# Products over 64 and 32 rows of the array made over all rows, and the output projection in chunks of 512, 320 and 256 columns, in a hybrid decoder step

## The chip, the core and the metric

The kernel runs on one core of a Trainium2 chip. The core has TensorE (PE in the profile; its loads of weights are PEld), VectorE (DVE), ScalarE (ACT), GpSimd (POOL) and SyncE (SP), which issues nearly all transfers. The metric is the device time of one execution in microseconds (us).

## The reference, cut to what matters

One layer of a decoder (D_MODEL 2048) for a prompt of 1024 tokens and for 8 sequences of 8 new tokens (64 in all; 1088 tokens together):

```python
h = rmsnorm(x) * (1 + scale) + shift                 # scale, shift, gate from silu(c) @ ada_w
q_a, k_a, v_a, z_a, u_b, v_b, z_b, qk_c, v_c, o_c, z_c, i_c, f_c = split(h @ w_in)
# A, 12 heads of 64: q, k normalised in each head; three dilated windows with relative bias,
#    combined by their softmax denominators; times silu(z_a)
# B, spatial gating: u * (tril(w_s) @ rmsnorm(v) + b_s) * silu(z_b)
# C, mLSTM, 6 heads of 128: short causal conv on q/k, chunkwise recurrence with
C_new = wc * C + einsum('bhs,bshk,bshv->bhkv', ws, k, v)
x = x + gate * (concat(y_a, y_b, y_c) @ w_out)
```

All of it is in float32. It returns the new x, and the new windows, buffers and states.

## The kernel before, in words

Data lies with features on the 128 partitions and the 1088 tokens along the row. Large products are made of three: an operand is split into a high part, rounded to the format that TensorE multiplies at the higher rate (float32r, FR in the code), and a low part, the rest; high*high + high*low + low*high are added in one PSUM bank. `products` (L249) issues these three, lines 252, 253 and 254, for one block of 128 input features and one chunk of tokens. The tokens are cut into three chunks, `CH` (L25): 384, 384 and 320.

ACT rounds the high part of a weight piece (L98), POOL makes the low part (L99), both two pieces ahead; SP loads pieces still further ahead (L87).

Stages in order: norm and modulation, with the first columns of the input projection accumulated as the modulation arrives (to 200 us); columns of the input projection (`column`, L602: a tile of 128 output features over four weight pieces and three chunks); the mLSTM heads beside later columns (to 1215 us); spatial gating; the attention of the new tokens against the cache, beside further columns (1525 to 1910 us); the first part of the output projection (features 6 to 15 of `yD`, `project`, L1586) with the prompt's attention woven in (to some 2395 us); the second part (features 0 to 5, the attention's own output).

The order is written out by hand. After each group of products `tick` (L179) lets background work take steps: `hp` one step at each tick, `lp` `rate` steps (0.345 a tick in the first part of the projection). Work in `lp` is written as generators, and each `yield` ends a step. Each engine works off its own instructions in this order, so a step fixes only the order, and semaphores the rest. Stores are put off by some ticks (`later`, L157).

Products over fewer than 128 rows that the diff touches:

- Norm factors of q and k, `rms` (L757). The sums of squares of both heads of a tile end up at rows 32c and 32c+1 of chunk c, 96 rows for the three chunks (L762); DVE takes the inverse root, keeps it as a rounded and a remaining part in the rows 32c to 32c+3 (`yc`, L781), and a product with the selector `sel` (L787), over the 32 rows of the chunk, spreads it over the 128 features. `sel` is 96 x 128 (L258), loaded at the very start (L263). Twelve tiles, three chunks.
- States of the new tokens, in `mlstm` (L909): the update of the state for four sequences at once, 512 columns. `kwh` holds the high part of the weighted keys twice, in rows 0 to 63 and 64 to 127; `vm` holds the values, high part above, low part below; L1032 multiplies over 128 rows, L1033 multiplies the low part of the keys, `kwl` (64 rows), with the upper half of `vm`. Six heads, two halves.
- Scores of the prompt's attention, `scores` (L1428): `qs` holds the high part of q in rows 0 to 63 and its low part in 64 to 127; `kd` holds the high part of k twice. L1442 makes high*high + low*high over 128 rows, L1443 adds high*low over rows 0 to 63 with `kl` (L1403). Columns: up to 512 keys, at least 256. 144 such pairs, 12 for each of the 12 heads.

Around the scores, in one step: the products of probabilities with values, L1493 and L1495, for an earlier block; the scores of a block; the transposes of an earlier block's probabilities (`turn`, L1470, L1484); then what is due (exp, scaling L1459, the low part `pL` of the transposed probabilities L1486). `prep` (L1383) loads and splits keys, queries and values of the next head, for heads after the first on POOL (L1403, L1408, L1414).

`project` (L1586) keeps three PSUM banks, one for each chunk, and `residual` (L1575) adds gate * result to x, in the last chunk with a part of its own for the 64 new tokens.

Other lines named later: L276 and L762 (sums of squares), L346 and L357 (modulation), L1242 and L1292 (scores and values of the new tokens), all of which write 32 output partitions; L287 to L289 (transposes of 96, 64 and 32 rows in `token_rsqrt`); L1061 (transposes in `mlstm`).

Of the kernel before, what the change touches and what calls it, by code (L numbers as in the profile page):

```python
# [11 lines left out]
FT = mybir.dt.float32  # L12
FR = mybir.dt.float32r
# [98 lines left out]
def body(tc, I, O):  # L112
# [20 lines left out]
    def et(name="e"):  # L133
        return ev.tile([128, 388], FT, tag="e", name=name, bufs=7)
# [122 lines left out]
    gate = cp.tile([128, KT, ND9], FT, name="gate")  # L257
    sel = cp.tile([96, 128], FR, name="sel")  # L258
    knew = cp.tile([128, 2, 2, NSM], FT, name="knew")
    qg8 = cp.tile([128, 1], FT, name="qg8")  # L260
    V.tensor_scalar(qg8, C("qg"), 0.125, None, op0=OP.mult)
    t = et("sel")
    SP.dma_start(t[:96, :128], I["sel"][:96])  # L263
    V.tensor_copy(sel, t[:96, :128])

# [489 lines left out]


    def rms(cc, g, emit):  # L757

        yield
        ps = bank("rq")  # L760
        for c, (t0, n) in enumerate(CH):
            T.matmul(ps[32 * c:32 * c + 32, :n], C("half"), cc[c][1][:, :n], start=True, stop=True, skip_group_check=True)  # L762
        a = cc[0][1]
        V.tensor_scalar(a[0:64, :384], ps[0:64, :384], 1.0 / 64, EPS, op0=OP.mult, op1=OP.add)
        V.tensor_scalar(a[64:96, :320], ps[64:96, :320], 1.0 / 64, EPS, op0=OP.mult, op1=OP.add)
        V.memset(a[64:96, 320:384], 1.0)
        y, t = et("y")[:96, :384], et("t")[:96, :384]
        a = a[:96, :384]
        V.tensor_scalar(y.bitcast(I32), a.bitcast(I32), -0.5, 1597463007.0, op0=OP.mult, op1=OP.add)
        for i in range(3):  # L770
            if i < 2:
                yield
            V.tensor_tensor(t, y, y, op=OP.mult)
            V.scalar_tensor_tensor(t, t, -0.5, a, op0=OP.mult, op1=OP.mult)
            V.scalar_tensor_tensor(y, t, 1.5, y, op0=OP.add, op1=OP.mult)

        yh, yc = (ev.tile([128, 388], FR, tag="e", name=x, bufs=7)[:96, :384] for x in ("yh", "yc"))
        yield
        S.copy(yh, y)
        yield  # L780
        V.scalar_tensor_tensor(yc, y, C("low", rows=96), yh.bitcast(FT), op0=OP.mult, op1=OP.subtract)  # L781
        yield
        for c, (t0, n) in enumerate(CH):
            raw = cc[c][0]
            ps = bank("rb")
            r = slice(32 * c, 32 * c + 32)
            T.matmul(ps[:, :n], sel[r, :], yc[r, :n], start=True, stop=True)  # L787
            V.scalar_tensor_tensor(raw[:, :n], raw[:, :n], g, ps[:, :n], op0=OP.mult, op1=OP.mult)
            emit(c, raw, t0, n)
            yield  # L790
# [45 lines left out]
    pcv = mp_.tile([128, 12, 3], FT, name="pcv")  # L836
    scv = mp_.tile([128, 12, NB, 3], FT, name="scv")
    pnt = mp_.tile([128, HC], FT, name="pnt")
# [31 lines left out]
    def h_qk(h, isk):  # L870
# [3 lines left out]
        def f(c, ps, t0, n):  # L874
# [19 lines left out]
            if c == 2:  # L894
# [4 lines left out]
                for j in range(1, 4):  # L899
                    V.scalar_tensor_tensor(us, Rs[:, :, j:j + NT], cw[:, m, j:j + 1], us, op0=OP.mult, op1=OP.add)  # L900
                V.tensor_copy(scv[:, m], Rs[:, :, 8:11])
            S.activation(t[:, :n], u[:, :n], AF.Tanh)
# [6 lines left out]
    def mlstm(h):  # L909
# [97 lines left out]
        kv = ev.tile([128, 388], FR, tag="e", name="kvp", bufs=7)  # L1007
        kwh, vns, kwl = kv[:, 0:128], kv[:, 128:256], kv[:p, 256:384]
        S.copy(kwh[:p], kw[:p])
# [5 lines left out]
        T.matmul(b3[:, 256:264], kw[:p], C("bm01", rows=p), start=True, stop=True)  # L1015
        V.tensor_tensor(kwl, kw[:p], kwh[:p].bitcast(FT), op=OP.subtract)
        V.tensor_tensor(vns[p:], vn[:p, :128], vns[:p].bitcast(FT), op=OP.subtract)
# [4 lines left out]
        for i in range(2):  # L1022
# [9 lines left out]
            T.matmul(b3, kwh, v2, start=True, stop=False)  # L1032
            T.matmul(b3, kwl, v2[:p], start=False, stop=True)  # L1033
            V.tensor_tensor(c, c, b3.rearrange("p (b v) -> p b v", b=4), op=OP.add)
# [46 lines left out]
    for p in range(2, 4):  # L1081
        column(col["va", p], h_va(p))
    column(col["ka", 0], h_qka(0, True))
    drain(lp)
    later(lambda: (SP.dma_start(O["p_conv"], pcv), SP.dma_start(O["s_conv"], scv),
                   SP.dma_start(O["p_n"], pnt), SP.dma_start(O["s_n"], snt)))
# [126 lines left out]
    def sample(qd):  # L1213
# [18 lines left out]
        for hf in range(2):  # L1232
# [65 lines left out]
            for b in range(4):  # L1298
                T.matmul(os_[32 * b:32 * b + 32, :256], pts[5][:NSM, 32 * b:32 * b + 32], vn, start=False, stop=True,
                         skip_group_check=True)  # L1300
            ost = ap_.tile([128, 256], FT, tag="ost", name="ost", bufs=1)
            S.copy(ost, os_[:, :256])
# [80 lines left out]
    def prep(hd):  # L1383
# [18 lines left out]
        S.copy(kd[:, :NPR], kr[:, :NPR])  # L1402
        E.tensor_tensor(kl[0:64, :NPR], kr[0:64, :NPR], kd[0:64, :NPR].bitcast(FT), op=OP.subtract)  # L1403
        e["kd"], e["kl"] = kd, kl
# [23 lines left out]
    def scores(e, m):  # L1428

        P = []  # L1430
        for r in range(2):
# [6 lines left out]
            for k0 in range(0, nk, 512):  # L1438
# [3 lines left out]
                T.matmul(ps[:, :wide], e["qs"][:, a], e["kd"][:, k0:k0 + wide], start=True, stop=False)  # L1442
                T.matmul(ps[:, :wide], e["qs"][0:64, a], e["kl"][0:64, k0:k0 + wide], start=False, stop=True)  # L1443
                x = k0 + 896 - 128 * qb
# [122 lines left out]
    def loads(ks):  # L1567
        for j, k in enumerate(ks):
# [4 lines left out]
            load_y(k, G)  # L1573

    def residual(x, c, ps, t0, n, dm):  # L1575
        npr = n if c < 2 else n - NSM
# [9 lines left out]
    def project(pieces, src, dst):  # L1586
        for dm in range(KT):
# [3 lines left out]
            for q, (k0, nk) in enumerate(pieces):  # L1591
                wh, wl = W.get()
                last = q == len(pieces) - 1
                for c, (t0, n) in enumerate(CH):
                    if q == 0:
# [187 lines left out]
```

## Time and profile before

| | |
|---|---|
| median of 3 runs | 2551.05 us (2546.61 to 2551.82) |
| the profiled execution, whole | 2550.13 us |
| its span, first to last instruction | 2548.4 us |
| TensorE busy in the span | 2499.6 us (98%) |
| DVE, ACT, POOL busy | 940.8, 746.1, 645.7 us (37%, 29%, 25%) |
| mean granted clock of TensorE | 0.995 |
| matmuls | 15879 |

How to read it: a row of the timeline gives the start in us from the span's start, the duration in us, the engine, the line of the kernel, the operation, output<-inputs by their names in the program, and for a matmul rows*columns of the loaded weights, then rows x columns of the moving operand; x4 is four in a row, merged. Matmuls overlap: the next one starts before the one ahead has ended, so their durations add up to more than the time. In the row of granted clocks each digit is a fortieth of the span, in tenths. In a list of waits a row is: who waited, line, for whom, us in total, times, the longest.

### The profile page before, as it was taken

Reading aid. Unit: us, or ns where it says so; the run is one execution under the profiler, and the core shown is the slowest. Engines: PE = TensorE matmul, PEld = TensorE weight load, DVE = VectorE, ACT = ScalarE, POOL = GpSimd, SP = SyncE. Lnnn points to the kernel's source line nnn. Section 1 sums busy time; section 2 is a strip of 40 time slices with the busy share of each in tenths; the row PEclk is TensorE's granted clock in tenths of the full one; section 3 lists DMA queues with packets and bytes.
Section 4 is the critical chain, followed back from the end, with each engine's and each line's share of the span. In section 5 each row is a group of like instructions: output and inputs, shape, how many; then the busy total and the mean of one; then the engine's idle time right before and its main releaser. Section 6 shows DMA issues by size and latency. Waiting matters only on the chain.

```text
span 2548.4 us, 39820 instructions
## 1 busy us (share of the span) xinstructions
PE 2499.6 (98%) x15879; PEld 2264.7 (89%) x15879; DVE 940.8 (37%) x2480; ACT 746.1 (29%) x1638; POOL 645.7 (25%) x502
## 2 busy tenths in 40 slices
PE   5999999999999999999999999999999999999999
PEld 2677899999999999999899998888889888888999
DVE  4673001323232323232440003333113777777322
ACT  3222212323232323223221112222113555555210
POOL 2541123222323131312212221111111323232421
PEclk8999999999999999999999999999999999999999
DMA  8864611111112111112314327475657455444454
GB/s 282 283 215 157 216 57 38 60 55 59 60 55 65 55 60 55 56 59 78 96 59 132 113 89 257 170 235 198 232 181 229 120 137 143 141 140 131 146 170 144
DMA packets 157081, 332.95 MB, mean 131 GB/s; under 512 B 21770, under 2 KB 76962, under 8 KB 149216
## 3 DMA queue, kind: packets, MB, share of 16 engines
q1 hardware_dynamic: 156896, 330.41, 40.0%
q8 instruction: 125, 2.05, 0.3%
q14 instruction: 60, 0.49, 0.1%
HBM read 284.26 MB, written 54.55 MB: 133 GB/s over the span
## 4 chain that ended last, share of the span: by engine, by line
PE 93%; DMA 3%; DVE 3%; issue 0%; SPq 0%; ACT 0%; POOL 0%; DVEq 0%; ACTq 0%; POOLq 0%
PE mm L252 26%; PE mm L254 25%; PE mm L253 25%; PE pt L1484 2%; PE s L1443 2%; PE ad L346 2%; PE os L1292 1%; PE s L1442 1%; PE sq L1242 1%; PE o L1495 1%; PE o L1493 1%; DMA x<-in_xT 1%; PE rb L787 1%; DMA ad<-in_adaw 0%; PE b L936 0%; PE b L968 0%
## 5 line engine op out<-in xcount | busy, mean ns | idle before, releaser
L252 PE MATMUL mm<-hH,wh 128*128 128x384 f32 (+1 forms) x3168 | 1066.5, 337 | 10.5 <-ACT hH L429 8.5
L253 PE MATMUL mm<-hL,wh 128*128 128x384 f32 (+1 forms) x3168 | 1034.9, 327 | 2.5 <-DVE hL L435 2.5
L254 PE MATMUL mm<-hH,wl 128*128 128x384 f32 (+1 forms) x3168 | 1036.3, 327 | 0.0
L99 POOL TENSOR_TENSOR wl<-wraw,wh 128x512 fp32r<-128x512 f32 x344 | 444.0, 1298 | 1619.8 <-ACT wh L98 1477.1
L252 PEld LDWEIGHTS mm<-hH,wh 128*128 128x128 f32 x3168 | 595.4, 188 | 80.9 <-issue 46.4
L253 PEld LDWEIGHTS mm<-hL,wh 128*128 128x128 f32 x3168 | 595.9, 188 | 4.2 <-DVE hL L435 3.6
L254 PEld LDWEIGHTS mm<-hH,wl 128*128 128x128 f32 x3168 | 595.1, 188 | 0.0
L98 ACT CAST wh<-wraw 128x512 fp32r<-128x512 f32 x344 | 200.9, 596 | 381.8 <-PE mm L253 276.6
L252 PE MATMUL mm<-yH,wh 128*128 128x384 f32 (+1 forms) x768 | 264.3, 344 | 2.8 <-DVE xo L1577 2.8
L254 PE MATMUL mm<-yH,wl 128*128 128x384 f32 (+1 forms) x768 | 252.2, 328 | 0.6 <-POOL wl L99 0.6
L253 PE MATMUL mm<-yL,wh 128*128 128x384 f32 (+1 forms) x768 | 251.8, 328 | 0.0
L252 PEld LDWEIGHTS mm<-yH,wh 128*128 128x128 f32 x768 | 145.1, 189 | 6.1 <-issue 5.9
L254 PEld LDWEIGHTS mm<-yH,wl 128*128 128x128 f32 x768 | 145.0, 189 | 0.9 <-POOL wl L99 0.9
L253 PEld LDWEIGHTS mm<-yL,wh 128*128 128x128 f32 x768 | 145.6, 190 | 0.0
L892 DVE SCALAR_TENSOR_TENSOR u<-R,cw,u 128x384 f32<-128x384 f32 (+1 forms) x108 | 62.0, 574 | 213.3 <-ACT u L890 210.8
L1485 ACT CAST pH<-pt 128x512 fp32r<-128x512 f32 (+1 forms) x120 | 65.2, 544 | 125.3 <-PE pt L1484 124.4
L1577 DVE SCALAR_TENSOR_TENSOR xo<-mm,gate,xo 128x384 f32<-128x384 f32 (+1 forms) x96 | 54.3, 569 | 117.0 <-PE mm L254 116.7
L1486 DVE TENSOR_TENSOR pL<-pt,pH 128x512 fp32r<-128x512 f32 (+1 forms) x120 | 75.3, 628 | 17.0 <-ACT pH L1485 15.0
L1484 PE MATMUL pt<-cst,P 128*128 128x128 f32 x432 | 75.0, 290 | 3.1 <-DVE P L1459 2.6
L1445 DVE CUSTOM_DVE_ANT_0 P<-s,btab 128x512 f32<-128x512 f32 (+2 forms) x96 | 56.4, 587 | 57.0 <-PE s L1443 54.9
L1454 ACT ACTIVATE P<-P,mx 128x128 f32<-128x128 f32 (+3 forms) x96 | 74.4, 776 | 4.0 <-DVE mx L1451 2.1
L1484 PEld LDWEIGHTS pt<-cst,P 128*128 128x128 f32 x432 | 45.9, 141 | 27.9 <-issue 17.2
(323 smaller groups left out, 2422.4 us busy)
## 6 DMA issues: line engine op xcount, KB each, us to landing
wraw<-in_win SPq DMA_DIRECT2D x264, 256.0 KB
ad<-in_adaw SPq DMA_DIRECT2D x96, 512.0 KB
kv<-in_ck SPq DMA_DIRECT2D x30, 1024.0 KB
kv<-in_cv SPq DMA_DIRECT2D x30, 1024.0 KB
wraw<-in_wout SPq DMA_DIRECT2D x48, 256.0 KB
x<-in_xT SPq DMA_DIRECT2D x16, 544.0 KB
yraw<-yD SPq DMA_DIRECT2D x16, 544.0 KB
xo<-in_xT SPq DMA_DIRECT2D x16, 544.0 KB
```

The costliest lines, as they stand in the source:

```text
L98: self.nc.scalar.copy(wh[:, :n], raw[:, :n])
L99: self.nc.gpsimd.tensor_tensor(wl[:, :n], raw[:, :n], wh[:, :n].bitcast(FT), op=OP.subtract)
L252: T.matmul(ps[:, :n], wh[:, a], rh[:, t0:t0 + n], start=first and i == 0, stop=False)
L253: T.matmul(ps[:, :n], wh[:, a], rl[:, t0:t0 + n], start=False, stop=False)
L254: T.matmul(ps[:, :n], wl[:, a], rh[:, t0:t0 + n], start=False, stop=last and i == len(rows) - 1)
L892: V.scalar_tensor_tensor(u[:, :npr], R[:, j:j + npr], cw[:, m, j:j + 1], u[:, :npr], op0=OP.mult, op1=OP.add)
L1445: V.tensor_tensor_reduce(s[:, k0:k0 + w], ps[:, :w], e["bt"][:, x:x + w], 1.0, mx[:, np_ - 1:np_] if np_ else -3.0e38, op0=OP.add, op1=OP.max,
L1454: S.activation(s[:, :nk], s[:, :nk], AF.Exp, bias=mx[:, 2:3], accum_out=mx[:, 3:4])
L1484: T.transpose(pt[:, o:o + 128], P[r][:, k:k + 128], ident)
L1485: S.copy(pH[:, f:], pt[:, f:])
L1486: at(0, 3, lambda: V.tensor_tensor(pL[:, f:], pt[:, f:], pH[:, f:].bitcast(FT), op=OP.subtract))
L1577: V.scalar_tensor_tensor(x[:, t0:t0 + npr], ps[:, :npr], gate[:, dm, 0:1], x[:, t0:t0 + npr], op0=OP.mult, op1=OP.add)
```

## The change

It makes three kinds of product over all rows of the array instead of a part of them, and cuts the projection's chunks otherwise.

- `sel` becomes three blocks of 96 x 128, each zero but for the 32 rows of its chunk; L787 then multiplies over all 96 rows. `sel` is loaded, zeroed and filled after the start stage's memory is given back (about 305 us in the profile before) instead of at the start.
- `kwl` is made for both halves of the rows, so L1033 multiplies over 128 rows (the low part of the keys times the low part of the values comes in besides).
- `kl` is made for 128 rows, so L1443 multiplies over 128 rows (low*low comes in besides).
- `project` uses `CO`, chunks of 512, 320 and 256, instead of `CH`.
- For room: the updated conv buffer is written in place (`sconv` instead of `scv`), and `ost` takes a buffer of the ring `pt`.

```diff
-    sel = cp.tile([96, 128], FR, name="sel")
-    t = et("sel")
-    SP.dma_start(t[:96, :128], I["sel"][:96])
-    V.tensor_copy(sel, t[:96, :128])
@@ after st0.close()
+    sel = pool("qk", bgs, bufs=1).tile([96, 3, 128], FR, name="sel")
+    t = et("sel")
+    SP.dma_start(t[:96, :128], I["sel"][:96])
+    V.memset(sel.bitcast(FT), 0.0)
+    for c in range(3):
+        r = slice(32 * c, 32 * c + 32)
+        V.tensor_copy(sel[r, c, :], t[r, :128])
@@ rms
-            r = slice(32 * c, 32 * c + 32)
-            T.matmul(ps[:, :n], sel[r, :], yc[r, :n], start=True, stop=True)
+            T.matmul(ps[:, :n], sel[:, c, :], yc[:, :n], start=True, stop=True)
@@ h_qk
-                V.tensor_copy(scv[:, m], Rs[:, :, 8:11])
+                V.tensor_copy(sconv[:, m], Rs[:, :, 8:11])
@@ mlstm
-        kwh, vns, kwl = kv[:, 0:128], kv[:, 128:256], kv[:p, 256:384]
+        kwh, vns, kwl = kv[:, 0:128], kv[:, 128:256], kv[:, 256:384]
-        V.tensor_tensor(kwl, kw[:p], kwh[:p].bitcast(FT), op=OP.subtract)
+        for r in (slice(0, p), slice(p, 128)):
+            V.tensor_tensor(kwl[r], kw[:p], kwh[:p].bitcast(FT), op=OP.subtract)
-            T.matmul(b3, kwl, v2[:p], start=False, stop=True)
+            T.matmul(b3, kwl, v2, start=False, stop=True)
@@ sample
-            ost = ap_.tile([128, 256], FT, tag="ost", name="ost", bufs=1)
+            ost = ap_.tile([128, 256], FT, tag="pt", name="ost", bufs=3)
@@ prep
-        E.tensor_tensor(kl[0:64, :NPR], kr[0:64, :NPR], kd[0:64, :NPR].bitcast(FT), op=OP.subtract)
+        E.tensor_tensor(kl[:, :NPR], kr[:, :NPR], kd[:, :NPR].bitcast(FT), op=OP.subtract)
@@ scores
-                T.matmul(ps[:, :wide], e["qs"][0:64, a], e["kl"][0:64, k0:k0 + wide], start=False, stop=True)
+                T.matmul(ps[:, :wide], e["qs"][:, a], e["kl"][:, k0:k0 + wide], start=False, stop=True)
@@ project
+    CO = ((0, 512), (512, 320), (832, 256))
-                for c, (t0, n) in enumerate(CH):
+                for c, (t0, n) in enumerate(CO):
```

More of the change, by code (lines that the diff above doesn't have):

```diff
@@ L836, in body @@
     pcv = mp_.tile([128, 12, 3], FT, name="pcv")
-    scv = mp_.tile([128, 12, NB, 3], FT, name="scv")
     pnt = mp_.tile([128, HC], FT, name="pnt")
@@ L1084, in body @@
     drain(lp)
-    later(lambda: (SP.dma_start(O["p_conv"], pcv), SP.dma_start(O["s_conv"], scv),
+    later(lambda: (SP.dma_start(O["p_conv"], pcv), SP.dma_start(O["s_conv"], sconv),
                    SP.dma_start(O["p_n"], pnt), SP.dma_start(O["s_n"], snt)))
```

## The prediction

> **What bounds the kernel now.** I read the page first: the busy shares, the row of granted clocks, then the waits of TensorE, then the timeline of TensorE around every kind of product that the diff touches.
>
> ```profile
> span 2548.4 us, 39820 instructions
> PE 2499.6 (98%) x15879; PEld 2264.7 (89%) x15879; DVE 940.8 (37%) x2480; ACT 746.1 (29%) x1638; POOL 645.7 (25%) x502
> PEclk8999999999999999999999999999999999999999
> ```
>
> TensorE is busy 98% of the span at nearly full granted clock. A busy PE isn't a PE at its peak, so the question is what lies inside the busy time. The waits of TensorE over the stage where prompt attention is woven into the first part of the output projection (1955 to 2395 us), and the engines' busy time there:
>
> ```profile
> PE mm L252 <- DVE xo L1577: 2.8, 1, 2.8
> PE pt L1484 <- DVE P L1459: 2.6, 3, 1.5
> PE o L1495 <- DVE pL L1486: 0.8, 3, 0.4
> ```
>
> ```profile
> 1960.00:2395.00 435.00, 429.23 (x2515) 369.19 (x2516) 311.05 (x922) 241.36 (x495) 130.18 (x83) 0.99 0.49 139
> ```
>
> The columns of the second are the stretch, then busy us and instructions of PE, PEld, DVE, ACT and POOL, the clock, the DMA share and GB/s. TensorE waits for others some 6 us in 440; everything else that it loses, it loses to itself. So I price each product by the distance from its start to the next start, which the timeline gives, and not by its duration (a matmul that lasts 0.33 us starts 0.17 us after the one before). The measure for undisturbed products, from the second part of the projection, fifteen products of 384 columns and then twelve of 320:
>
> ```profile
> 2537.01 0.33 PE L252 MATMUL mm<-yH,wh 128*128 128x384 f32 x1
> ...
> 2539.61 0.31 PE L252 MATMUL mm<-yH,wh 128*128 128x320 f32 x1
> ...
> 2541.36 0.34 PE L252 MATMUL mm<-yH,wh 128*128 128x384 f32 x1
> ```
>
> (2539.61 - 2537.01)/15 = 0.173 us for 384 columns, (2541.36 - 2539.61)/12 = 0.146 for 320: 0.0275 per 64 columns. Carried on, that gives 0.228 for 512 and 0.118 for 256 (an estimate for 512: no undisturbed one is in the trace).
>
> **The change part by part.** (a) Norm factors, L787, 32 rows. How many of each touched product there are, and one of them with its neighbours (rows*columns of the loaded weights, then rows x moving columns):
>
> ```profile
> L787 PE MATMUL rb<-yc,sel x36: 403/436/442, 1226.1 to 1787.0; 32*128 32x384 f32 x24, 32*128 32x320 f32 x12
> L1443 PE MATMUL s<-kl,qs x144: 379/466/501, 1964.8 to 2356.8; 64*128 64x512 f32 x72, 64*128 64x256 f32 x48, 64*128 64x384 f32 x24
> L1033 PE MATMUL b<-vm,kvp x12: 492/498/502, 512.6 to 1187.3; 64*128 64x512 f32 x12
> ```
>
> ```profile
> 1225.88 0.31 PE L254 MATMUL mm<-hH,wl 128*128 128x320 f32 x1
> 1226.12 0.44 PE L787 MATMUL rb<-yc,sel 32*128 32x384 f32 x1
> 1226.49 0.45 PE L252 MATMUL mm<-hH,wh 128*128 128x384 f32 x1
> 1226.77 0.34 PE L253 MATMUL mm<-hL,wh 128*128 128x384 f32 x1
> ```
>
> Three distances are too long. Before it: 0.24 where 0.146 is due (+0.094). Its own: 0.37 for 0.173 (+0.197). The one behind: 0.28 for 0.173 (+0.107). Together 0.40 us for one product over 32 rows, besides its own stream. After the change the product has 96 rows. Does 96 still count as a part of the array? The trace has one product over 96 rows behind a full one:
>
> ```profile
> 1241.09 0.34 PE L254 MATMUL mm<-hH,wl 128*128 128x384 f32 x1
> 1241.27 0.33 PE L287 MATMUL tr<-cst,ts 96*128 96x96 f32 x2
> ```
>
> 0.18 us before it, as between full ones; so I take 96 rows as full. Along the timeline 15 of the 36 are followed by a full product of the projection (0.40 each: 6.0 us), 9 by full products of 128 columns, behind which the third distance is over by 0.06 only, as (b) shows (0.35 each: 3.2), and 12 by products into 32 output columns. Those have a distance of their own in front:
>
> ```profile
> 1528.32 0.34 PE L254 MATMUL mm<-hH,wl 128*128 128x384 f32 x1
> 1528.59 1.07 PE L1242 MATMUL sq<-kv,qst 128*32 128x256 f32 x16
> ```
>
> 0.27 where 0.173 is due. So of the 0.197 behind these twelve L787 only 0.10 goes, and 0.09 ahead: 0.19 each, 2.3 us. Sum of (a): 11.5 us.
>
> (b) Scores, L1443, 64 rows. One pair of 512 columns with four transposes behind it, the same four transposes behind a full product, and one pair of 384 columns with a projection product behind it:
>
> ```profile
> 2202.58 0.40 PE L1442 MATMUL s<-kd,qs 128*128 128x512 f32 x1
> 2202.90 0.50 PE L1443 MATMUL s<-kl,qs 64*128 64x512 f32 x1
> 2203.33 0.66 PE L1484 MATMUL pt<-cst,P 128*128 128x128 f32 x4
> 2203.75 0.42 PE L252 MATMUL mm<-yH,wh 128*128 128x384 f32 x1
> ```
>
> ```profile
> 525.70 0.34 PE L254 MATMUL mm<-hH,wl 128*128 128x384 f32 x1
> 525.87 0.60 PE L1061 MATMUL b<-cst,kT 128*128 128x128 f32 x4
> 526.23 0.43 PE L252 MATMUL mm<-hH,wh 128*128 128x384 f32 x1
> ```
>
> ```profile
> 2196.89 0.28 PE L1495 MATMUL o<-pL,vh 128*64 128x256 f32 x1
> 2197.01 0.34 PE L1442 MATMUL s<-kd,qs 128*128 128x384 f32 x1
> 2197.28 0.43 PE L1443 MATMUL s<-kl,qs 64*128 64x384 f32 x1
> 2197.64 0.44 PE L252 MATMUL mm<-yH,wh 128*128 128x384 f32 x1
> 2197.92 0.34 PE L253 MATMUL mm<-yL,wh 128*128 128x384 f32 x1
> ```
>
> With transposes behind: L1442 to L1443 0.32 for 0.228, L1443 to L1484 0.43 for 0.228, the four transposes 0.42 for 0.36: +0.09, +0.20, +0.06, in all 0.35. With a projection product or the next pair behind: 0.27 for 0.173, 0.36 for 0.173, 0.28 for 0.173: in all 0.39. Counted along the timeline, 115 of the 144 are of the first kind and 29 of the second: 40.3 + 11.3 = 51.6 us. The full-row L1443 itself costs what L1442 costs: the columns are the same. L1495 (128 rows, 64 columns of weights) has 0.12 behind it, which is undisturbed, so it isn't touched and needn't be.
>
> (c) States, L1033, 64 rows, 512 columns, projection products behind: 0.09 + 0.20 + 0.11 = 0.40, twelve times, 4.8 us.
>
> So 11.5 + 51.6 + 4.8 = 67.9 us come off TensorE, and since TensorE is the end of nearly every step of the chain, off the time, except where somebody else is late instead.
>
> (d) What is late next. In the attention stage DVE has 311 us in what would be 383 (435 - 52), 81%, and its worst moments come from long POOL work beside it:
>
> ```profile
> 2206.86 2.40 POOL L1403 TENSOR_TENSOR kl<-kr,kd 64x1024 fp32r<-64x1024 f32 x1 [8.82 <-ACT kd L1402]
> 2206.97 3.81 DVE L1459 TENSOR_SCALAR P<-P,mx 128x512 f32<-128x512 f32 x1
> 2210.70 0.68 DVE L1486 TENSOR_TENSOR pL<-pt,pH 128x512 fp32r<-128x512 f32 x1
> 2211.43 0.33 PE L1495 MATMUL o<-pL,vh 128*64 128x256 f32 x1
> ```
>
> A DVE scaling took 3.81 us while POOL split keys and then weights; pL was ready at 2211.38, and TensorE took it at 2211.43: 0.05 us to spare. Between a pT and its product lie two steps of the weave, each shorter by one pair's 0.35; so TensorE comes 0.70 us earlier and waits about that. One such meeting in each of 12 heads: 8.4 us, which I take. The ends: nothing (the meetings where nobody is late have more to spare), and three for each head, one for each of POOL's three splits (L1403, L1408, L1414): 25 us.
>
> (e) Chunks of 512, 320, 256 for 384, 384, 320: the same 1088 columns and the same three chunks. New 0.228 + 0.146 + 0.118 = 0.492, old 0.173 + 0.173 + 0.146 = 0.492: nothing. The loads of weights do not bind at 256: 0.12 stands behind L1495, and a load of 128 columns lies in it. Both new widths are uncertain by some 0.006 us, over 768 products of each chunk: 5 us either way. The ticks of the weave grow uneven (three products of 0.228, then of 0.146, then of 0.118), so steps in the narrow chunk are shorter by 2.9 ticks x 3 x 0.028 = 0.24 us; that is inside the 25 us. The smaller last chunk takes a part of 0.1 us off the tail.
>
> (f) Edits at nothing. kl over 128 rows: POOL's duration goes with elements in a row (2.40 us over 64 rows here), so the same; without that cover (POOL's idle time) 11 x 2.4 us of POOL would be late. kwl twice instead of once: DVE is idle most of that stage, and two yields lie before its use. sconv written in place, ost in another ring: no new wait, since each earlier reader is done long before. sel moved from the start to 305 us, past the first loads of x:
>
> ```profile
> 1.26 0.41 SPq L263 DMA_DIRECT2D sel<-in_sel  x1
> ```
>
> This issue leaves the head of SP's queue (at most its 0.41 us gained; I count none). At its new place its load and DVE's zeroing and three copies stand ahead of the first heads' work, DVE waiting for the load; behind it queue only operations that are needed a column or two later, and SP's next weight loads run pieces ahead. Zero, at most 3 us if a weight piece comes late.
>
> A rule of the Trainium skill speaks against the change: "TensorE: Matmul & The Clock Gate", section Why this matters for your kernels, advises giving products over few rows row groups of their own, so that they run at once. The trace answers for this kernel: L787 and L1443 have full products on both sides and take 0.24 to 0.43 us for distances of 0.146 to 0.228; nothing runs beside them. By the rule the full rows would lose an overlap (last rival below); by the rows there is none to lose.
>
> **The sum.** 67.9 off, 8.4 back: 59.5 us. The profiled execution took 2550.13 us, and becomes 2490.6; the median of the runs, 2551.05, lies 0.9 above it, so the forecast is 2492. Its bounds: 67.9 + 5 off gives 2478; 25 + 5 + 3 back gives 2516.
>
> **The rivals.** *DVE, slowed by POOL, becomes the bound of attention.* For it: 81% busy, 3.81 us in one operation. Against it: TensorE waits only 6 us there today, and five banks and two steps lie between. If half or all of the 51.6 us turn into waits: 2551 - 68 + 26 = 2509 to 2535. Chance 0.12. *It isn't the rows:* the gap at L1443 and L1033 comes from a second product into the same bank; then only (a) goes, 2540. Against it: L252 to L253 write one bank at 0.173, and L787, alone in its bank, has the same three gaps. 0.03. *Slower: 512 columns are dear by themselves.* If the 0.32 us behind the 512 columns of L1442 were their own price, each of 768 products would cost 0.09 more, 69 us, and the 0.09 ahead of 84 products would stay: 2492 + 69 + 8 = 2569. It decides from 0.077 us more per wide product (59.5/768). Against it: the excess ahead of a partial product is 0.09 to 0.10 at 320, 384 and 512 alike. 0.03. *Slower: lost overlap.* Were the partial products hidden beside neighbours, their streams would be added, 72 x 0.228 + 24 x 0.173 + 48 x 0.118 = 26 us for L1443, 24 x 0.173 + 12 x 0.146 = 6 for L787, 12 x 0.228 = 3 for L1033: 2586. Against it: the excess around each of them, which is the opposite of an overlap. 0.01. (It is the case that the page of the Trainium skill named above would have.)
>
> **How the numbers follow.** The forecast has 0.81. 2478 to 2516 takes its bounds in and the near end of the first rival. About 0.2% is what a measurement here can tell from no change. Faster by more than that: 0.81 + 0.12 + 0.03, less 0.01 for the far ends: 0.95; within 0.01; slower 0.04.
>
> **What would show it.** L1442 to L1443 at 0.23 for 512 columns and L1443 to L1484 at 0.23; 0.15 to 0.17 around L787; 0.27 kept where a product into 32 columns follows; PEld no longer idle ahead of L1443; the attention stage near 390 us; waits for P and pL of 5 to 25 us; three chunks of projection at 0.228, 0.146, 0.118. Wrong, if gaps stay at L1443 or L787, if 512 columns take over 0.30, or if waits in attention exceed 30 us.

## The result, and the profile after

The changed kernel takes 2487.3 us (median of 4 runs, 2486.51 to 2489.15), the kernel before 2550.26 (4 runs, 2546.61 to 2551.82): 0.9756 of the time, 95% interval 0.9739 to 0.9773, or 63 us less. The forecast was 2492. The page of the changed kernel:

```profile
span 2487.2 us, 39837 instructions
PE 2435.5 (98%) x15879; PEld 2228.4 (90%) x15879; DVE 939.0 (38%) x2489; ACT 746.2 (30%) x1638; POOL 646.5 (26%) x502
```

The span is 61.2 us shorter, and the busy time of TensorE 64.1, with the same number of products. DVE, ACT and POOL do the same work as before: the busy share of TensorE (98% both times) could not show what was lost inside it.

Lines have moved: L787 is L790, L1032 and L1033 are L1035 and L1036, L1442 and L1443 are L1445 and L1446, L1484 is L1487, L1493 and L1495 are L1496 and L1498, L1242 is L1245; in the rows of waits L1459 is L1462, L1485 and L1486 are L1488 and L1489, L1577 is L1583. First a norm factor with its neighbours, in the timeline of the changed kernel:

```profile
1220.29 0.31 PE L254 MATMUL mm<-hH,wl 128*128 128x320 f32 x1
1220.44 0.34 PE L790 MATMUL rb<-yc,sel 96*128 96x384 f32 x1
1220.61 0.34 PE L252 MATMUL mm<-hH,wh 128*128 128x384 f32 x1
1220.79 0.33 PE L253 MATMUL mm<-hL,wh 128*128 128x384 f32 x1
```

0.15, 0.17, 0.18 us from start to start, where 0.24, 0.37, 0.28 stood before: the product over 96 rows is an ordinary one. Where a product into 32 columns follows, its own entry stays:

```profile
1572.03 0.34 PE L790 MATMUL rb<-yc,sel 96*128 96x384 f32 x1
1572.30 0.64 PE L1245 MATMUL sq<-kv,qst 128*32 128x256 f32 x8
```

0.27 for 384 columns, as predicted. The states, and a pair of scores with four transposes behind:

```profile
511.95 0.39 PE L1035 MATMUL b<-vm,kvp 128*128 128x512 f32 x1
512.18 0.39 PE L1036 MATMUL b<-vm,kvp 128*128 128x512 f32 x1
512.41 0.34 PE L252 MATMUL mm<-hH,wh 128*128 128x384 f32 x1
```

```profile
2197.56 0.39 PE L1445 MATMUL s<-kd,qs 128*128 128x512 f32 x1
2197.79 0.40 PE L1446 MATMUL s<-kl,qs 128*128 128x512 f32 x1
2198.02 0.60 PE L1487 MATMUL pt<-cst,P 128*128 128x128 f32 x4
2198.38 0.36 PE L252 MATMUL mm<-yH,wh 128*128 128x256 f32 x1
```

0.23 and 0.23 for 512 columns (0.32 and 0.43 before), 0.36 for the transposes (0.42 before). The load of weights for the second product, which itself starts at 2202.90 in the kernel before and at 2197.79 in the changed one:

```profile
2202.90 0.18 PEld L1443 LDWEIGHTS s<-kl,qs 64*128 64x128 f32 x1 [0.31 <-issue]
2197.56 0.19 PEld L1446 LDWEIGHTS s<-kl,qs 128*128 128x128 f32 x1
```

Over 64 rows the load starts together with its product (all 144 within 0.003 us), over 128 rows ahead of it, here by 0.23 us and together with the product before (0.11 to 0.24 us in the 144). The new chunks, undisturbed, in the second part of the projection:

```profile
2474.68 0.40 PE L252 MATMUL mm<-yH,wh 128*128 128x512 f32 x1
...
2477.43 0.30 PE L252 MATMUL mm<-yH,wh 128*128 128x320 f32 x1
...
2479.19 0.28 PE L252 MATMUL mm<-yH,wh 128*128 128x256 f32 x1
...
2480.62 0.40 PE L252 MATMUL mm<-yH,wh 128*128 128x512 f32 x1
```

Twelve of each: 0.229, 0.147, 0.119. The waits of TensorE over the attention stage (1925 to 2345 us):

```profile
PE pt L1487 <- DVE P L1462: 5.9, 6, 1.5
PE mm L252 <- DVE xo L1583: 2.8, 1, 2.8
PE o L1498 <- DVE pL L1489: 1.8, 4, 1.1
PE o L1496 <- ACT pH L1488: 1.2, 1, 1.2
PE mm L254 <- POOL wl L99: 1.1, 1, 1.1
PE pt L1487 <- DVE mx L1448: 0.3, 1, 0.3
```

13.1 us in all. Of the kernel before the prediction shows 6.2; with the rows that it leaves out (0.4, 0.2 and one of 0.6 for wl) it was 7.4. So 5.7 us of what was won is waited away. The first part of the projection, to the start of the second, takes 414.7 us instead of 457.8, 43.1 less.

I added up the distances from each product's start to the next start, by what the product is (us; "behind" is the distance of the product that follows):

| | before | after | difference |
|---|---|---|---|
| ahead of the norm factors, their own, behind | 10.74, 12.86, 5.72 | 7.45, 7.21, 3.62 | -11.0 |
| first and second product of the scores | 41.19, 54.99 | 26.50, 27.33 | -42.4 |
| behind the scores, waits for P in it | 25.64 | 21.32 | -4.3 |
| first and second product of the states, behind | 3.97, 5.13, 3.35 | 2.84, 2.79, 2.10 | -4.7 |
| output projection | 394.74 | 395.47 | +0.7 |
| input projection | 1609.41 | 1607.32 | -2.1 |
| all else | 367.24 | 370.69 | +3.5 |
| sum | 2534.98 | 2474.64 | -60.3 |

"All else" holds the products with values, where the waits for pL and pH stand. The two traces also differ in clock: the kernel before gets half the clock of TensorE for 3.4 us twice in the first part of the projection (from 1961.2 and from 2367.4 us), the changed kernel once (from 1944.1). Half of 3.4 us, so some 1.7 of the 60.3, is clock by this estimate.

### The profile page after: what moved, and what is told of

Its sections match the earlier page's. It is cut to its first block, busy times and chain, and to the rows that moved or that the text cites. A ratio compares the mean times of both kernels' runs of the same rounds, so it can differ in the third digit from the quotient of the medians.

```text
span 2487.2 us, 39837 instructions
## 1 busy us (share of the span) xinstructions
PE 2435.5 (98%) x15879; PEld 2228.4 (90%) x15879; DVE 939.0 (38%) x2489; ACT 746.2 (30%) x1638; POOL 646.5 (26%) x502
## 4 chain that ended last, share of the span: by engine, by line
PE 91%; DVE 3%; DMA 3%; issue 1%; ACT 1%; SPq 1%; POOL 0%; DVEq 0%; ACTq 0%; POOLq 0%
PE mm L252 26%; PE mm L254 25%; PE mm L253 25%; PE ad L342 2%; PE pt L1487 2%; PE os L1295 1%; PE sq L1245 1%; PE o L1498 1%; PE s L1446 1%; PE o L1496 1%; PE s L1445 1%; DMA x<-in_xT 1%; DMA ad<-in_adaw 1%; PE b L938 0%; PE b L970 0%
## 5 line engine op out<-in xcount | busy, mean ns | idle before, releaser
L252 PE MATMUL mm<-hH,wh 128*128 128x384 f32 (+1 forms) x3168 | 1063.2, 336 | 10.0 <-ACT hH L425 8.4
L252 PEld LDWEIGHTS mm<-hH,wh 128*128 128x128 f32 x3168 | 595.5, 188 | 75.3 <-issue 40.0
L252 PE MATMUL mm<-yH,wh 128*128 128x512 f32 (+2 forms) x768 | 262.3, 341 | 2.8 <-DVE xo L1583 2.8
L254 PE MATMUL mm<-yH,wl 128*128 128x512 f32 (+2 forms) x768 | 252.3, 329 | 1.1 <-POOL wl L99 1.1
L253 PE MATMUL mm<-yL,wh 128*128 128x512 f32 (+2 forms) x768 | 252.4, 329 | 0.0
L252 PEld LDWEIGHTS mm<-yH,wh 128*128 128x128 f32 x768 | 145.4, 189 | 12.2 <-issue 3.0
L1583 DVE SCALAR_TENSOR_TENSOR xo<-mm,gate,xo 128x512 f32<-128x512 f32 (+2 forms) x96 | 54.3, 568 | 116.1 <-PE mm L254 107.8
L1488 ACT CAST pH<-pt 128x512 fp32r<-128x512 f32 (+1 forms) x120 | 65.2, 543 | 81.1 <-PE pt L1487 80.4
L1489 DVE TENSOR_TENSOR pL<-pt,pH 128x512 fp32r<-128x512 f32 (+1 forms) x120 | 74.1, 618 | 15.6 <-ACT pH L1488 15.5
L1487 PE MATMUL pt<-cst,P 128*128 128x128 f32 x432 | 68.9, 274 | 6.3 <-DVE P L1462 5.9
L1487 PEld LDWEIGHTS pt<-cst,P 128*128 128x128 f32 x432 | 52.7, 140 | 19.3 <-DVE P L1462 9.2
```

The lines of the kernel that those rows point to most:

```text
L252: T.matmul(ps[:, :n], wh[:, a], rh[:, t0:t0 + n], start=first and i == 0, stop=False)
L253: T.matmul(ps[:, :n], wh[:, a], rl[:, t0:t0 + n], start=False, stop=False)
L254: T.matmul(ps[:, :n], wl[:, a], rh[:, t0:t0 + n], start=False, stop=last and i == len(rows) - 1)
L1487: T.transpose(pt[:, o:o + 128], P[r][:, k:k + 128], ident)
L1488: S.copy(pH[:, f:], pt[:, f:])
L1489: at(0, 3, lambda: V.tensor_tensor(pL[:, f:], pt[:, f:], pH[:, f:].bitcast(FT), op=OP.subtract))
```

## The experiments

Two theories at first. A: a product over part of the rows costs a gap ahead, one of its own and one behind, whatever it computes. B: the gaps at scores and states come from the second product into the same bank. Later ones: D, that POOL's splits hold up DVE and so make the new waits in attention; and for the chunks, that they are neutral, dear, or make waits. "Before" was measured beside the kernels of each group again: 2549.79, 2549.96, 2550.79 and 2550.27 us.

**The scores alone.**

```diff
-    E.tensor_tensor(kl[0:64, :NPR], kr[0:64, :NPR], kd[0:64, :NPR]...)
+    E.tensor_tensor(kl[:, :NPR], kr[:, :NPR], kd[:, :NPR]...)
-    T.matmul(ps, e["qs"][0:64, a], e["kl"][0:64, k0:k0 + wide], ...)
+    T.matmul(ps, e["qs"][:, a], e["kl"][:, k0:k0 + wide], ...)
```

> The kernel before with the scores alone made over all rows (kl for 128 rows, L1443 over 128 rows); all else as before. Theory A (a product over part of the rows costs 0.35 to 0.40 us of gaps ahead of it, of its own and behind it): 51.6 us off TensorE, some 5 back as waits in attention, so 45 to 50 us less than before; L1442 to L1443 at 0.23 for 512 columns. Rival B (the gap comes from the second product into one bank, not from the rows): no change, L1442 to L1443 stays at 0.32.

2506.11 us, 0.9828 (0.9812 to 0.9844): 43.7 less. B falls: the bank and the second product are the same, only the rows changed. The sums of the two products fell from 41.19 and 54.99 to 26.71 and 27.50. The median is a little under 45 to 50 (the interval, 39.8 to 47.9, reaches into it). The waits (1950 to 2350 us) rose to 13.6 from 7.4 us, 6.2 where I said some 5:

```profile
PE pt L1484 <- DVE P L1459: 6.4, 8, 1.5
PE mm L252 <- DVE xo L1577: 3.7, 1, 3.7
PE o L1495 <- DVE pL L1486: 1.5, 4, 0.8
PE o L1493 <- ACT pH L1485: 1.4, 2, 1.2
```

**The norm factors alone.**

```diff
+    sel = pool("qk", bgs, bufs=1).tile([96, 3, 128], FR, name="sel")   # zeroed, three blocks filled, after st0
-    T.matmul(ps[:, :n], sel[r, :], yc[r, :n], start=True, stop=True)
+    T.matmul(ps[:, :n], sel[:, c, :], yc[:, :n], start=True, stop=True)
```

> The kernel before with the norm factors alone made over 96 rows (sel as three zero-padded blocks, loaded and filled at its later place; with it the two edits that make room: sconv in place, ost in the ring of pt). Theory A: 11.5 us less than before (the profile after showed 11.0 around these products), the move of sel and the two edits costing nothing. Rival (sel at its later place delays weights or DVE): less than 8 us, with a wait of TensorE between 300 and 320 us. Rival B as well expects 11.5 here, since these products are alone in their bank.

2536.22 us, 0.9943 (0.9928 to 0.9958): 13.6 less, with 11.5 inside the interval. There is no wait of TensorE at the new place of `sel`. The rest of 2 us lies, in the profile as in that of the whole change, in the input projection (1607.58 for 1609.41 us). It goes with this edit: all ten kernels that have it take 1606.2 to 1608.3 us there, the four without it 1609.4 to 1611.1. Which part of the edit makes it (the load gone from the start, the products over 96 rows, the two edits for room) is not shown. The granted clock of these runs is also a little higher (mean 0.9965 of 6, for 0.9956 of 23), some 2 us by an estimate; the interval is too wide to tell the two apart.

**The states alone.**

```diff
-    V.tensor_tensor(kwl, kw[:p], kwh[:p].bitcast(FT), op=OP.subtract)
-    T.matmul(b3, kwl, v2[:p], start=False, stop=True)
+    for r in (slice(0, p), slice(p, 128)):
+        V.tensor_tensor(kwl[r], kw[:p], kwh[:p].bitcast(FT), op=OP.subtract)
+    T.matmul(b3, kwl, v2, start=False, stop=True)
```

> The kernel before with the states alone made over all rows (kwl for both halves, L1033 over 128 rows). Theory A: 4.8 us less than before, 0.2%, at the limit of what can be told; in the profile L1032 to L1033 0.23 for 0.33, L1033 to the next 0.23 for 0.43. Rival B: no change, and these distances stay. A second DVE subtraction in each head that delays the product would show as a wait ahead of L1032: none expected.

2545.05 us, 0.9979 (0.9967 to 0.9990): 4.7 less (2.5 to 8.4). The sums around them fell from 3.97, 5.13 and 3.35 to 2.87, 2.81 and 2.09, 4.7 us; no wait came with the second subtraction.

**The chunks alone.**

```diff
+    CO = ((0, 512), (512, 320), (832, 256))
-    for c, (t0, n) in enumerate(CH):
+    for c, (t0, n) in enumerate(CO):
```

> The kernel before with the chunks of the projection alone cut 512, 320, 256. Theory A: within 5 us of before, either way; undisturbed distances 0.228, 0.146, 0.118 in the second part. Rival (512 columns dear by themselves): 69 us more. Rival (uneven steps of the weave make waits in attention): 5 to 25 us more, seen as waits for P and pL over the 4 us of before.

2553.28 us, 1.0013 (1.0004 to 1.0022): 3.5 more. Not dear by themselves: the second part of the projection, from its first product to the last start of an L252, takes 142.28 us with the old chunks and 142.36 with the new. In the profiles the loss lies in the first part (462.4 for 457.8 us), but the waits there hardly differ: 3.2 us for the first residual, 2.8 for P, 1.2 for pL, 7.2 in all. What differs is the clock. Both kernels get half of it around the wait for the first residual, the kernel before for 3.4 us and this one for 10.2 (columns as in the prediction; the clock is the third figure from the end):

```profile
1961.20:1964.60 3.40, 2.98 (x9) 3.01 (x10) 1.54 (x5) 1.45 (x3) 1.49 (x2) 0.50 0.76 204
1965.80:1976.00 10.20, 9.29 (x23) 6.82 (x23) 2.93 (x11) 2.54 (x7) 3.20 (x3) 0.50 0.76 216
```

That is 3.4 of the 4.6 us between the profiles. Over all runs the mean granted clock is 0.9949 here (12 runs) and 0.9956 before (23), which by an estimate makes some 1.7 of the 3.5 us. So neither rival explains the loss; a part of it is clock, and the rest stays open.

**The changed kernel with the old chunks.** One line of `project` goes back.

```diff
-                for c, (t0, n) in enumerate(CO):
+                for c, (t0, n) in enumerate(CH):
```

> The changed kernel with the projection's chunks as before (384, 384, 320); all rows in the three products. The four single edits gave -43.7, -13.6, -4.7 and +3.5 us, in sum -58.5; the whole change gave some -62.5. Theory A (the edits add up, chunks cost 3.5 by themselves): 2484, that is 3 to 4 us below the changed kernel, 66 below before. Rival (with short scores the uneven chunks help, the wide chunk giving DVE and ACT room): 2490 to 2492, some 4 us above the changed kernel, and more waits for P and pL than its 9 us.

2488.79 us, 0.9756 (0.9742 to 0.9771), where the changed kernel has 0.9756 (0.9739 to 0.9773): no difference. Its first part takes 414.4 us, the changed kernel's 414.7. In the medians the chunks neither help nor hurt once the scores go over all rows. The profiles are again uneven in clock: half of it for 6.8 us with the old chunks, for 3.4 in the changed kernel. Taking off half of each, the first part is 411.0 with the old chunks and 413.0 with the new; in the kernel before and the chunks alone the same reckoning gives 454.4 and 455.6. By these single profiles the new chunks cost 1 to 2 us in both places, which the medians here can't tell from nothing.

**Splits on DVE.**

```diff
-        E = G if hd else V
+        E = V
-        G.tensor_tensor(vh[:, :, 1, :], vs, vh[:, :, 0, :].bitcast(FT), op=OP.subtract)
+        V.tensor_tensor(vh[:, :, 1, :], vs, vh[:, :, 0, :].bitcast(FT), op=OP.subtract)
```

> The changed kernel with the three splits of prep (keys, queries, values) on DVE instead of POOL, for every head. Theory D (POOL's splits stretch DVE's scalings beside them, and that makes the waits for P and pL): the scalings of 512, 768 and 1024 columns fall back to 0.49, 0.62 and 0.75 us but for those beside weight splits, TensorE's waits in attention fall from 13 us below 8, and the time by 3 to 6 us against the changed kernel. Rival (DVE's work itself is what TensorE waits for): 37 us more on DVE raise the waits, and the time is 5 to 15 us longer than the changed kernel.

2515.87 us, 0.9869 (0.9853 to 0.9886): 28.6 more than the changed kernel, beyond what either said. Neither is settled by it, since a third thing came in. The group of DVE's split of keys (busy, mean ns, idle time ahead), and TensorE's waits:

```profile
L1406 DVE TENSOR_TENSOR kl<-kr,kd 128x1024 fp32r<-128x1024 f32 x12 | 15.0, 1247 | 30.4 <-ACT kd L1405 30.4
```

```profile
PE pt L1487 <- DVE mx L1448: 9.5, 7, 2.7
PE pt L1487 <- DVE P L1462: 8.8, 9, 1.5
PE mm L252 <- DVE xo L1583: 6.1, 1, 6.1
```

The scalings did fall back as theory D has it: 10 of 12 over 512 columns take 0.49 us, 9 of 12 over 768 take 0.62, 9 of 12 over 1024 take 0.75. But DVE works in order: it stands still 30 us in all for ACT's casts of the keys, and the scaling, the maxima and the residual queue behind it. TensorE waits 29.4 us in this stage, for 13.1 in the changed kernel, and has half the clock for 20.5 us of it, where the changed kernel has that for 3.4: by an estimate these two come to some 25 us, and the span of the profile is 23.6 longer. A wait that POOL could afford is not affordable on DVE.

**Without the splits of keys and queries.**

```diff
-        kd, kl = slot("kd", FR), slot("kl", FR)
+        kd, kl = slot("kd", FR), zero[0]
-        E.tensor_tensor(kl...)
-        E.tensor_tensor(qs[64:128, :NPR]...)
```

> The changed kernel without the splits of keys and queries in prep, in place of an attempt that moved them to DVE and so made DVE wait for ACT's casts (30 us ahead of the split of keys). Left out: the low part of the keys (a tile of zeroes in its place) and of the queries (the rows hold the high part a second time); all products stay. Theory D (POOL's splits hold up DVE operations that read only SBUF, and that makes the waits for P, pL and pH): TensorE's waits for these in attention fall from 9.2 us to below 5, the scaling t*z at 0.42 us instead of 0.70 mean, and the time is 4 to 6 us below the changed kernel. Rival (the steps are simply too short for the chain scores, exp, scaling): waits stay at 8 to 10 us, time within 2 us of the changed kernel.

2479.54 us, 0.9715 (0.9702 to 0.9728): 7.8 less than the changed kernel. The waits for P fell from 5.9 to 1.7, those for pL and pH stayed (1.8 and 1.4), and the wait for the first residual (2.8), which stands behind the first head's splits, went. The waits for the three are 4.9 us, as expected just below 5. The mean of t*z fell only from 0.70 to 0.58 us, not to 0.42: the splits of values and of weights are still on POOL, and it still takes 2.48 us once. So the splits do make waits, but the kernel also leaves out work of DVE (the first head's splits), so this run alone doesn't separate the two.

**Inputs from PSUM.** Here the work stays, and only its inputs change (on top of the kernel "more products" below).

```diff
-    V.tensor_tensor(t, po[0][0:64, :256], t, op=OP.add)
-    V.scalar_tensor_tensor(t, t, 0.5, e["z"]..., op0=OP.mult, op1=OP.mult)
+    w = po[0][0:64, 256:512]
+    V.tensor_tensor(w, po[0][0:64, :256], t, op=OP.add)
+    V.scalar_tensor_tensor(t, w, 0.5, e["z"]..., op0=OP.mult, op1=OP.mult)
-    u = tp.tile([128, NB, NT], FT, tag="u", name="u", bufs=1)
+    u = ps[:, npr:n].rearrange("p (b t) -> p b t", b=NB)
```

> The kernel with more products over the full array (2485.5 us) and two DVE operations of the attention stage given one input from PSUM instead of two from SBUF: the sum of the two halves of o is written to PSUM, so t*z (mean 0.70 us, alone 0.42) reads it there, and the gated new-token part of the residual is made in place in PSUM. Nothing is left out. Theory D: t*z falls to 0.45 us mean beside POOL, the last part of the residual below 0.3; waits for P and pL fall by 2 to 4 us; 2481 to 2484. Rival (only the scalings of P matter): waits unchanged, 2485 to 2487.

2479.35 us, 0.9716 (0.9702 to 0.9729); its base is at 0.9747 (0.9733 to 0.9762). What it cured, in the timeline of the changed kernel:

```profile
2199.21 2.41 POOL L1411 TENSOR_TENSOR qs<-qr,qs 64x1024 fp32r<-64x1024 f32 x1 [2.15 <-ACT qs L1410]
2199.29 2.61 DVE L1507 SCALAR_TENSOR_TENSOR t<-t,zt 64x256 f32<-64x256 f32 x1
2203.41 1.25 POOL L1417 TENSOR_TENSOR vh<-vr,vh 128x512 fp32r<-128x512 f32 x1
2203.56 1.52 DVE L1462 TENSOR_SCALAR P<-P,mx 128x768 f32<-128x768 f32 x1
2205.14 0.55 PE L1487 MATMUL pt<-cst,P 128*128 128x128 f32 x3 [1.44 <-DVE P L1462]
```

DVE's t*z, 256 columns, lasts 2.61 us and ends 0.28 us after POOL's split of queries. All of DVE is late by that; the scaling of P is held up once more (1.52 us for 768 columns, 0.62 alone) by the split of values, and TensorE waits 1.44 us. It is no single case: of the 48 t*z of the changed kernel, 34 have no POOL instruction beside them and take 0.42 us; the other 14 overlap one, take 0.51 to 2.61 us, and each ends 0.27 to 0.28 us after an instruction of POOL has ended. The group of t*z in the changed kernel, and in the one with inputs from PSUM (busy, mean ns, idle time ahead):

```profile
L1507 DVE SCALAR_TENSOR_TENSOR t<-t,zt 64x256 f32<-64x256 f32 x48 | 33.4, 696 | 1.7
```

```profile
L1513 DVE SCALAR_TENSOR_TENSOR t<-o,zt 64x256 f32<-64x256 f32 x48 | 20.0, 417 | 1.6
```

From 0.42 to 2.61 us each before, now all 48 between 0.416 and 0.418; the last parts of the residual (0.22 to 1.74 before) all take 0.22. The waits, same stage:

```profile
PE mm L252 <- DVE xo L1589: 2.9, 1, 2.9
PE pt L1492 <- DVE P L1467: 2.6, 3, 1.5
PE o L1501 <- ACT pH L1493: 1.2, 1, 1.2
PE o L1503 <- DVE pL L1494: 0.4, 2, 0.2
```

P from 5.9 to 2.6, pL from 1.8 to 0.4, and the time by 6.1 us, a little more than the 1.5 to 4.5 I expected. D holds, and this is its cheap cure. The two inputs were moved together, so what each of them is worth is not shown.

**The scaling in a form that writes a sum.**

```diff
-    V.tensor_scalar(s[:, :nk], s[:, :nk], mx[:, 4:5], None, op0=OP.mult)
+    V.tensor_scalar(s[:, :nk], s[:, :nk], mx[:, 4:5], 0.0, op0=OP.mult, op1=OP.add, accum_out=mx[:, 5:6])
```

> The one before this, and the scaling of P on DVE in a form that also writes a sum (not used). It is expected to run at half the rate, 0.35 us longer for 1024 columns, but not to be held up by POOL: durations of one length alike beside POOL and alone (now 0.49 to 2.7 us for 512 columns). If the hold-ups make the waits: waits for P below 3 us, 2 to 4 us less than the one before. Rival (DVE's own work makes them): 10 to 15 us more work on DVE, waits as before or more, time 0 to 5 us longer.

2479.68 us, 0.9718 (0.9704 to 0.9731): the same. The scalings of one length became alike, beside POOL and alone, but each is longer than one that nothing held up: for 512 columns 0.75 us (before this edit 0.49 to 2.70, mean 1.03), for 1024 columns 1.28 (0.75 to 1.38, mean 0.89; 0.53 longer than alone, where I expected 0.35). The waits for P are 2.3 us, for 2.6. So doing away with the hold-ups of the scaling gained nothing here. Either TensorE no longer waits for them, and what is left is the chain of scores, exp and scaling in a short step, or the longer scalings took back the gain; this run can't tell the two apart.

**Scores over 96 rows.**

```diff
-    T.matmul(ps, e["qs"][:, a], e["kl"][:, k0:k0 + wide], ...)
+    T.matmul(ps, e["qs"][0:96, a], e["kl"][0:96, k0:k0 + wide], ...)
```

> The changed kernel with the second product of the scores over rows 0 to 95 instead of all 128 (what is left out: low*low for 32 of the 64 features, a term that the kernel before left out altogether). Theory A2 (96 rows count as the full array): as the changed kernel within 3 us, L1445 to L1446 at 0.23 for 512 columns. Rival (any product over fewer than 128 rows pays): the gaps of 0.35 to 0.40 are back, 47 us longer than the changed kernel.

2490.09 us, 0.9764 (0.9750 to 0.9779), against 0.9756 for 128 rows: the same within the intervals, and far from 47 us more.

```profile
2198.67 0.39 PE L1445 MATMUL s<-kd,qs 128*128 128x512 f32 x1
2198.91 0.39 PE L1446 MATMUL s<-kl,qs 96*128 96x512 f32 x1
2199.14 0.60 PE L1487 MATMUL pt<-cst,P 128*128 128x128 f32 x4
```

0.24 and 0.23. Same operands, same bank, 96 rows instead of 64: the cost isn't one of idle rows, it comes with 64 and 32 rows.

**More products over the full array.** Padding rows are zeroed on DVE.

```diff
+    V.memset(A[p:], 0.0); V.memset(A[:p, p:], 0.0); V.memset(kw[p:], 0.0); V.memset(vn[p:], 0.0)
-    T.matmul(b3[:p, 0:129], A[:p, :p], vn[:p], start=True, stop=True)
-    T.matmul(b3[:, 256:264], kw[:p], C("bm01", rows=p), start=True, stop=True)
+    T.matmul(b3[:, 0:129], A, vn, start=True, stop=True)
+    T.matmul(b3[:, 256:264], kw, C("bm01"), start=True, stop=True)
-    T.transpose(b1[:, 0:NSM], nds, ident[:NSM, :NSM])
+    T.transpose(b1[:, 0:128], nds, ident)
```

> The changed kernel with three more products made over the full array: in the mLSTM of the new tokens the two products of 64 rows behind the scores (numerator and sum of keys) and the transpose of 64 rows of the result, each padded to 128 by rows that DVE zeroes. Theory A: two bursts in each of six heads lose 0.3 to 0.4 us each, 4 us below the changed kernel; distance ahead of them 0.15 to 0.17 instead of 0.24. Rival (DVE's zeroing delays them): a wait of TensorE there, no gain.

2485.46 us, 0.9747 (0.9733 to 0.9762): 1.8 below the changed kernel, which the intervals can't tell apart; the span of the profile is 3.5 us shorter. The distances show it plainly:

```profile
508.40 0.31 PE L254 MATMUL mm<-hH,wl 128*128 128x320 f32 x1
508.55 0.38 PE L1021 MATMUL b<-vn,E 128*128 128x129 f32 x2
508.77 0.29 PE L1022 MATMUL b<-cst,kw 128*128 128x8 f32 x2
508.91 0.42 PE L252 MATMUL mm<-hH,wh 128*128 128x384 f32 x1
```

0.51 us from the product ahead to the one behind; in the kernel before the same four starts were at 509.16, 509.40, 509.76 and 510.08, 0.92 us (0.91 in the changed kernel).

**The first head's splits on POOL**, on top of the inputs from PSUM:

```diff
-        E = G if hd else V
+        E = G
```

> The kernel with PSUM inputs (2479.4 us) and the splits of the first head's keys and queries on POOL like those of the other heads, instead of on DVE. In the profile of that kernel TensorE waits 2.9 us for the first residual, which stands on DVE behind the first head's splits, which wait for ACT's casts and these 8.3 us for the load of keys; the granted clock is lower for some us behind it. If the place on DVE makes that wait: it goes, and the time is 3 to 5 us less, about 2475.5. Rival (the load holds up whatever stands behind ACT's cast): the weights' parts, on ACT and POOL in the same queues, come late instead, the wait moves to them, and the time stays within 2 us.

2480.83 us, 0.9726 (0.9712 to 0.9740): no gain. The rival is right; the wait of 2.9 us for the first residual is gone, and that for the weights' low part on POOL has risen from 0.8 to 2.8:

```profile
PE mm L254 <- POOL wl L99: 2.8, 2, 2.1
```

In its trace ACT's cast of the first head's keys waits 8.62 us for their load, and POOL's split 11.38 us for the cast; the weights' low part stands behind that split. The load holds up whatever queue stands behind the cast.

The best version is the one with the inputs from PSUM: 2479.4 us, 71 less than before, and its interval (0.9702 to 0.9729) lies below that of the changed kernel (0.9739 to 0.9773).

## Why the prediction was right

- **(a) Norm factors**, 11.5 us: 11.0 by the distances, 13.6 (10.7 to 18) measured alone. That 96 rows count as full was right, here and in the scores.
- **(b) Scores**, 51.6: the two rows of the table on the scores give 46.7, with 3.2 us more of waits for P in the second, so 49.9. Right.
- **(c) States**, 4.8: 4.7 by the distances, and 4.7 (2.5 to 8.4) alone.
- **(d) What is late next**, 8.4 us of 0 to 25: 5.7. The mechanism, POOL holding up DVE, is shown by the two kernels that took it away. The place was not the one I picked, and that the size came near is in part luck. I had TensorE wait for pL, 0.70 us in each of 12 heads, behind a scaling of P that was held up; the waits for pL rose by 1.0 us, those for P by 3.3. And the operation that mattered most in the changed kernel was t*z: curing it, together with the small residual part, took the waits for P and pL from 7.7 to 3.0 us, and the form of the scaling that POOL doesn't hold up took nothing more. The Trainium skill has the rule, in "SBUF — State Buffer", section Who interferes with whom: DVE and GpSimd share a port pair, which one instruction holds to its end, and DVE needs it for two SBUF inputs or in its faster modes of scaling, though not in the form that also writes an accumulated value. The traces agree: up to 2.61 us for 0.42 with two SBUF inputs, and then an end just behind the end of a POOL instruction; a constant 0.42 with one; a constant 0.75 in the form with the sum.
- **(e) Chunks**, nothing, 5 either way: the estimates 0.228, 0.146 and 0.118 came out at 0.229, 0.147 and 0.119, and the change with and without them is one time. Alone they cost 3.5 us (1 to 5.6); a part of that is clock, the rest stays open.
- **(f) Edits at nothing**: no wait anywhere that one of them would explain. But the input projection became some 2 us shorter with the norm factors' edit, the move of `sel` and the two edits for room among it, where I had nothing. POOL's split of keys over 128 rows takes 2.40 us, as over 64.
- **The sum**, 59.5: 60.3 by the distances, 63 by the medians. The terms err in both directions: 2.3 us too much gained in (a) to (c), 2.7 too much charged in (d), 2.1 us less in the input projection that I did not foresee; that would make 62.0, and 1.7 are given back in small amounts elsewhere. The clock, some 1.7 us in favour of the changed kernel, was not in the sum at all. The first part of the projection is 43.1 us shorter, which takes the 435 us of the attention stage to 392, near the 390 forecast.
- **The rivals.** DVE as the bound of attention: it took 5.7 us, not 26. The bank: refuted by the scores alone and by 96 rows. Dear wide products: 0.229 us. Lost overlap, which the page "TensorE: Matmul & The Clock Gate" of the Trainium skill would have: none of the three kinds of product was slower over all rows.

Why the rows cost anything: the Trainium skill's page "TensorEngine Tiling (Array Packing)", section Key Properties, says that changing the tiling mode drains TensorE; its section Available Configurations lists modes of 128, 64 and 32 rows. The traces agree (64 and 32 rows pay, 96 and 128 don't): a lone product between full ones cost 0.35 to 0.40 us. They show that the load of weights does not start early there (2202.90, with its product), but not what happens inside; the drain itself was not seen.

## What to carry to other kernels

Where one engine is busy all the time, read distances from start to start around each kind of its instructions, against an undisturbed stretch: 67.9 us of gaps were forecast so, one by one, in a busy share of 98%, and 65.6 were there. A lone product over 64 or 32 rows between full ones was cheaper here over all rows, with zeroes or harmless terms. Tiles can pay where several run in a row: the new tokens' scores (32 columns of weights each) start four at a time within 0.02 us, and 16 of them run in 1.07 us. When the bound engine is sped up, look at what else holds up its suppliers, and move an input (here to PSUM) before moving the work: the moved work cost 28.6 us, the moved input won 6.

## What the runs showed of the hardware that was not expected

- After a product over a part of the rows the second full product is late as well: 0.28 for 0.173 us. Why it lasts that long is not shown.
- A DVE operation can be held up across two POOL instructions in a row: 3.81 us for a scaling that takes 0.49 alone.
- The scaling with a sum takes 0.75 us for 512 columns and 1.28 for 1024, the plain one alone 0.49 and 0.75; steadier, and the kernel's time is the same.
- Widths are linear: 0.119, 0.147, 0.173, 0.229 us for 256, 320, 384, 512 columns, each product with its own load of 128 columns of weights.
